# Block 0's A12*B21 as a nested seven-product unit, with the sums of W2, the loads of x and some stores moved to make room for it

## The chip, the cores and the metric

One NeuronCore of one Trainium2 chip. The metric is device microseconds of one execution of the whole program.

## The reference

```python
x: 16 x 512 x 768, w1: 768 x 3072, b1: 3072, w2: 3072 x 768     # float32
y = x @ w1 + b1
y = 0.5 * y * (1 + erf(y / sqrt(2)))
out = y @ w2
```

## The kernel before

The 8192 rows are eight blocks of 1024. In each block the two matmuls are done by Strassen-Winograd: seven products of half-size operands (numbered 1 to 7) in place of eight, at the price of sums of operands, which VectorE makes. From block 2 on the second matmul is nested: each of the seven products is itself made by seven products of quarter size. Block 0's second matmul has one level only, in four row units; block 1's is mixed: its products 1, 4 and 2 are nested units ("UnitH"), and four "lean" row units do the other four. Nesting saves an eighth of the matrix work and costs sums, buffers and DRAM traffic, for which blocks 0 and 1 have little room.

A row unit of blocks 0 and 1, and its stores (shortened):

```python
class Unit2:                                   # one 128-row unit; sb is the block
    def __init__(self, g, sb, u):
        self.lean = sb > 0
    def mm(self, p, dst, first, c0, c1):       # product p: 12 matmuls of 384 columns
        if self.lean and p in (1, 2, 4):
            return                             # these come from the nested units
        ...
    def right_done(self):                      # upper row's store
        nc.sync.dma_start(out=orr[...], in_=self.o[:, 0, c0:N])
    def left_done(self, row, bank):            # ... lower row's sum or copy, then its store
```

A nested unit, one product of half size made by seven of quarter size:

```python
class UnitH(Unit3):
    def mm(self, q, dst, first, c0, c1):       # 12 matmuls of 192 columns for each q
        for c in range(NQ):
            for t in range(2):
                nc.tensor.matmul(out=dst[:, t * N4:(t + 1) * N4], lhsT=a, rhs=self.w[q][:, c, :], ...)
```

Units are interlaced. A period issues the first products of unit i between the last ones of unit j; between them stand six "slots", in which other engines' work is put into the program order:

```python
p1(i); copy_xy(i)            # ScalarE copies the start value into bank bY
p7(j); fill(1); p5(i); fill(2); p3(j); fill(3); p6(i); j.right_done(); fill(4)
p4(j); fill(5); p2(i); fill(6)            # lean row units: p5(i) ahead of p7(j), no p1, p2, p4
```

## Time and profile before

| | |
|---|---|
| median of the first runs | 852.89 us (852.71 to 853.48) |
| TensorE busy | 845.5 of 850.6 us |
| first product of block 0's second matmul | at 120.01 us |
| first product of block 2 | at 224.67 us |

Columns of a timeline: start in us, duration in us, engine, line, operation, output<-input, count, and in brackets how long the engine was idle before it and what released it. bX, bY, bZ and bW are PSUM banks, "arena" is the kernel's SBUF, and SPq or ACTq is a transfer issued by SyncE or ScalarE. Starts are exact; a matmul's end is modelled, so for TensorE I take differences of starts. A matmul of 384 columns starts 162.5 ns after its predecessor, one of 192 columns 82.5 ns.

### The profile page before, as it was taken

The numbers are of one execution on the slowest core, as the hardware profiler recorded it, in microseconds if no ns is written. First come the engines' busy times: TensorE is split into PE (matmuls) and PEld (weight loads), VectorE is DVE, ScalarE is ACT, GpSimd is POOL, SyncE is SP. The second block draws the span as 40 slices with busy tenths as digits, with TensorE's granted clock in tenths as the row PEclk, the third lists the DMA queues.
The fourth block names the chain that finished last, engine by engine and source line by source line (L and its number), as shares of the span: only waits on it lengthen the run. The fifth ranks groups of instructions, "written<-read, shape, count | busy, mean of one in ns | idle before, by whom it ended". The sixth has DMA issues, their size and how long they took to land.

```text
span 850.6 us, 16487 instructions
## 1 busy us (share of the span) xinstructions
PE 845.5 (99%) x6432; PEld 569.6 (67%) x6432; DVE 667.2 (78%) x1126; ACT 421.3 (50%) x686; POOL 84.1 (10%) x135
## 2 busy tenths in 40 slices
PE   9999999999999999999999999999999999999998
PEld 5444446687544897449964499645995469944798
DVE  5766678786657998679976799768996699956998
ACT  4777761122277513773148822487216771267611
POOL 5021100002100002000020000210002100010000
PEclk9999999999999999999999999999999999999999
DMA  9998777659999699987999689995999949984398
GB/s 229 199 284 170 165 160 277 234 195 218 234 331 207 194 332 372 296 177 236 332 381 266 155 291 335 361 293 111 315 351 344 283 111 328 356 311 172 101 310 283
DMA packets 143522, 219.05 MB, mean 258 GB/s; under 512 B 61756, under 2 KB 84724, under 8 KB 143444
## 3 DMA queue, kind: packets, MB, share of 16 engines
q1 hardware_dynamic: 117824, 179.74, 67.3%
q0 software_dynamic: 25440, 38.15, 20.6%
q8 instruction: 50, 0.82, 0.4%
q14 instruction: 28, 0.23, 0.1%
q10 hardware_dynamic: 180, 0.11, 0.0%
HBM read 180.30 MB, written 47.87 MB: 268 GB/s over the span
## 4 chain that ended last, share of the span: by engine, by line
PE 95%; DMA 4%; DVE 0%; ACT 0%; issue 0%; POOL 0%; DVEq 0%; ACTq 0%
PE bY L388 21%; PE bY L493 15%; PE bX L388 14%; PE bX L493 10%; PE bZ L388 7%; PE bW L388 7%; PE bZ L493 5%; PE bW L493 5%; PE bY L432 5%; DMA arena<-in_x_dram 2%; PE bZ L432 2%; PE bW L432 2%; PE bX L432 2%; DMA arena<-in_w_dram 1%; PE bY L580 1%; PE bX L580 1%
## 5 line engine op out<-in xcount | busy, mean ns | idle before, releaser
L191 DVE TENSOR_TENSOR arena<-arena 128x768 f16<-128x768 f16 (+4 forms) x630 | 403.4, 671 | 7.5 <-PE bW L432 1.1
L388 PEld LDWEIGHTS <-arena 128*128 128x128 f16 x1974 | 192.6, 98 | 224.0 <-issue 0.4
L493 PEld LDWEIGHTS <-arena 128*128 128x128 f16 x3528 | 292.1, 98 | 8.4 <-issue 0.4
L388 PE MATMUL bY<-arena 128*128 128x512 f16 x846 | 214.4, 379 | 0.1
L613 DVE TENSOR_TENSOR arena<-bY,arena 128x512 f32<-128x512 f32 (+1 forms) x102 | 69.4, 681 | 127.0 <-PE bY L388 90.3
L493 PE MATMUL bY<-arena 128*128 128x192 f16 x1500 | 138.3, 246 | 0.0
L388 PE MATMUL bX<-arena 128*128 128x512 f16 x564 | 138.2, 379 | 0.0
L606 ACT COPY bY<-bX 128x512 f32<-128x512 f32 (+1 forms) x143 | 78.6, 550 | 119.4 <-DVE arena L542 82.0
L404 ACT ACTIVATE arena<-arena,b1t 128x1024 f16<-128x1024 f32 x94 | 108.0, 1149 | 54.0 <-DVE arena L641 54.0
L626 ACT COPY arena<-bW 128x512 f32<-128x512 f32 (+1 forms) x147 | 81.1, 552 | 90.7 <-PE bW L493 43.9
L493 PE MATMUL bX<-arena 128*128 128x192 f16 x1020 | 93.1, 246 | 0.1
L641 DVE TENSOR_TENSOR arena<-bZ,arena 128x512 f32<-128x512 f32 (+1 forms) x102 | 69.3, 679 | 22.2 <-PE bZ L388 18.2
L388 PE MATMUL bW<-arena 128*128 128x512 f16 x282 | 76.2, 379 | 0.0
L388 PE MATMUL bZ<-arena 128*128 128x512 f16 x282 | 76.2, 379 | 0.0
L432 PEld LDWEIGHTS <-arena 128*128 128x128 f16 x528 | 51.6, 98 | 34.1 <-issue 0.2
L525 POOL DMA_DIRECT2D out_dram<-arena x42 | 30.6, 729 | 406.4 <-DVE arena L637 370.2
L409 ACT ACTIVATE arena<-bX,b1t 128x512 f16<-128x512 f32 x94 | 64.0, 681 | 10.0 <-PE bX L388 10.0
L409 ACT ACTIVATE arena<-bY,b1t 128x512 f16<-128x512 f32 x94 | 63.4, 674 | 0.0
L657 ACT COPY bZ<-bY 128x512 f32<-128x512 f32 (+1 forms) x54 | 29.0, 537 | 65.7 <-DVE arena L641 31.4
L299 POOL DMA_DIRECT2D arena<-in_x_dram x60 | 32.7, 550 | 248.2 <-DMA arena<-arena 137.9
L493 PE MATMUL bW<-arena 128*128 128x192 f16 x504 | 48.4, 246 | 0.0
L493 PE MATMUL bZ<-arena 128*128 128x192 f16 x504 | 48.4, 246 | 0.0
(60 smaller groups left out, 401.8 us busy)
## 6 DMA issues: line engine op xcount, KB each, us to landing
arena<-w2s SPq DMA_DIRECT2D x294, 288.0 KB, 4.7
arena<-w1s SPq DMA_DIRECT2D x72, 672.0 KB, 7.0
out_dram<-arena POOLq DMA_DIRECT2D x42, 384.0 KB, 7.2
w2s<-arena SPq DMA_DIRECT2D x49, 288.0 KB, 3.8
arena<-in_x_dram POOLq DMA_DIRECT2D x60, 192.0 KB, 7.1
w1s<-arena SPq DMA_DIRECT2D x12, 672.0 KB, 6.1
arena<-in_w_dram POOLq DMA_DIRECT2D x17, 384.0 KB, 7.6
out_dram<-arena SPq DMA_DIRECT2D x17, 384.0 KB, 3.4
```

The source lines that it names most:

```text
L191: nc.vector.tensor_tensor(out=o, in0=a, in1=b, op=op)
L299: nc.gpsimd.dma_start(out=xhs[t], in_=xr[:, sb * 8 + t, :])
L388: nc.tensor.matmul(out=dst[:, 0:RH], lhsT=w1_op(self.wt, slot)[:, c, :], rhs=a[:, c, :], start=first and c == 0, stop=c == self.C - 1, ski ...
L404: nc.scalar.activation(out=self.G[1][:, hi, :, :], in_=self.tmp, func=GELU, bias=b1t[:, 2 * hi + 1:2 * hi + 2])
L409: nc.scalar.activation(out=self.G[0][:, hi, row, :], in_=bank[:, 0:RH], func=GELU, bias=b1t[:, 2 * hi:2 * hi + 1])
L432: nc.tensor.matmul(out=dst[:, 0:N2], lhsT=a, rhs=w[:, :, c, :], start=first and c == 0, stop=c == self.C - 1, skip_group_check=True)
L493: nc.tensor.matmul(out=dst[:, t * N4:(t + 1) * N4], lhsT=a, rhs=w[:, c, :], start=first and c == 0 and t == ts[0], stop=c == NQ - 1, skip_ ...
L525: eng.dma_start(out=orr[:, s0:s0 + 2, right * N2:(right + 1) * N2], in_=self.dst[:, r].rearrange("p t h n -> p t (h n)"))
L606: nc.scalar.copy(out=bY[u.g % 2][:, 0:u.F], in_=bX[u.g % 2][:, 0:u.F])
L613: nc.vector.tensor_tensor(out=u.c22(), in0=bY[u.g % 2][:, 0:u.F], in1=w[:, 0:u.F], op=ADD)
L626: nc.scalar.copy(out=w[:, 0:u.F], in_=bW[:, 0:u.F])
L641: nc.vector.tensor_tensor(out=u.c12(), in0=bZ[:, 0:u.F], in1=w[:, 0:u.F], op=ADD)
```

## The change

Its intent: leave out product 2 of block 0's four row units and make it once, nested, ahead of block 1's three nested units. That costs buffers and time on VectorE just there, so the sums of W2 (28 of them, stored to DRAM for the later blocks) are spread over block 1 with five more buffers; six of these sums are fetched back from DRAM when they are needed; block 2's x is loaded sooner; the lean units' stores go from SyncE's queue to ScalarE's; and block 0's four copies from bY to bZ go from VectorE to ScalarE.

```diff
-            for n, a, b in ((7, b22, b12), ...):
-                    puts.append(lambda: put(n, t[n]))
+            for n, a, b in ((7, b22, b12), ...):
+                    puts.append([LAG[0], lambda eng: put(n, t[n], eng)])     # stored LAG slots later
...
+        HYBRID = ((0, 2), (1, 1), (1, 4), (1, 2))                             # was (1, 4, 2), block 1 only
...
+                self.eng = nc.scalar if self.lean and u < 2 * NU - 1 else nc.sync
...
-                if self.lean and p in (1, 2, 4):
+                if p == 2 or self.lean and p in (1, 4):
                     return
...
-                    for p in (5, 6, 7, 3):
-                        split_w2(p)
-                    hyb_w[1] = split_w2(1)
+                    for p, t in ((6, (0, 1, 2, 3)), (1, (4, 5, 0, 1)), (4, (2, 3, 4, 5)), (2, (0, 1, 2, 5))):
+                        split_w2(p, t)
...
             if m == 0 and slot == 1:
-                hyb_w[4] = split_w2(4, ...)
+                load_w2s(1, (7, 4))
...
+            if m == 1 and slot == 6:
+                split_w2(7, (6, 7, 8, 9))
+                split_w2(5, (10, 6, 7, 8))
...
-                if m == 2:
+                if m == 1:
                     load_next_x(2, range(3))
+                if m == 3:
+                    for t in range(3):
+                        transpose_dma(2, t)
+                    load_next_x(2, range(3, 6))
...
+            if k == 0 and slot == 4:
+                LAG[0] = 3
+                split_w2(3, (1, 2, 3, 4))
...
-            on_act = ... (isinstance(u, Unit2) and u.lean) ...                # copy bY -> bZ
+            on_act = ... isinstance(u, Unit2) ...
```

More of the change, by code (lines that the diff above doesn't have):

```diff
@@ L152 @@
     tmps1 = [tmp_at(o_tmp + 4 * k * RH) for k in range(2)]
-    o_stage = o_wt + 2 * WT_N
+    o_stage = o_wt + 2 * N + PAR
     stage = [cut(o_stage + k * WB, WB, "p (c n) -> p c n", c=NQ)
@@ L164, with strip, wb_at @@
           for o in (o_x0 + W2_N, o_x0 + W2_N + GS_N, o_x1, o_x1 + GS_N)]
-    osbs = [cut(o, PAR).bitcast(FP32).rearrange("p (a n) -> p a n", a=2)
-            for o in (o_wt, o_x1 + 2 * GS_N)]
-    par1, par4 = [cut(o, PAR).bitcast(FP32).rearrange("p (r t h n) -> p r t h n", r=2, t=2, h=2)
-                  for o in (o_wt, o_x1 + 2 * GS_N)]
+    osbs = [[cut(o, n).bitcast(FP32) for o, n in zip(oo, (2 * N2, 2 * N))]
+            for oo in ((o_x1 + 2 * GS_N + 2 * N + 2 * N2, o_wt),
+                       (o_x1 + 2 * GS_N + 2 * N, o_x1 + 2 * GS_N))]
+    assert 2 * N + 4 * N2 <= PAR
+    par02, par1, par4 = [cut(o, PAR).bitcast(FP32).rearrange(
+        "p (r t h n) -> p r t h n", r=2, t=2, h=2) for o in (o_wt + 2 * N, 2 * XT_N, o_x1 + 2 * GS_N)]
     par11 = cut(o_w2, W2P).bitcast(FP32).rearrange("p (c n) -> p c n", c=NH)[:, 0:8, 0:N4].rearrange(
         "p (r t h) n -> p r t h n", r=2, t=2)
-    osbs1 = [cut(XT_N + k * PAR, PAR).bitcast(FP32).rearrange("p (a n) -> p a n", a=2)
-             for k in range(2)]
-    def lev_strip(c, r):
-        return [Gs[0][k // 2][:, c:c + NQ, k % 2, r:r + 2 * P] for k in range(4)]
+    osbs1 = [[cut(XT_N + k * PAR, 2 * N2).bitcast(FP32),
+              cut(XT_N + k * PAR + 2 * N2, 2 * N).bitcast(FP32)] for k in range(2)]
+    def strip(h, a, c, r):
+        return Gs[0][h][:, c:c + NQ, a, r:r + 2 * P]
+    def wb_at(off):
+        return cut(off, WB, "p (c n) -> p c n", c=NQ)
+    hyb_lev = [[strip(0, 0, 0, 0), strip(1, 1, 0, 0), Gs[0][1][:, 0:NQ, 0, 2 * P:RH], strip(1, 1, NQ, 0)],
+               [strip(0, 1, 0, 0), strip(0, 0, NQ, 0), strip(0, 1, NQ, 0), strip(0, 0, 0, 2 * P)],
+               [strip(0, 1, 0, 2 * P), strip(0, 0, NQ, 2 * P), strip(0, 1, NQ, 2 * P), strip(0, 0, 0, 0)],
+               [strip(0, 1, 0, 0), strip(0, 0, NQ, 0), strip(0, 1, NQ, 0), strip(0, 0, NQ, 2 * P)]]
+    spare = stage + [wb_at(2 * XT_N + o) for o in
+                     (PAR, PAR + WB, XT_N, XT_N + WB, XT_N + 2 * WB)]
+    hyb_w = {2: {7: stage[0], 5: stage[1], 6: stage[2], 4: stage[5]},
+             1: dict(zip((7, 4, 5, 6), map(wb_at, (o_x0 + W2_N, o_x0 + W2_N + WB, o_x1, o_x1 + WB)))),
+             4: {7: wb_at(o_x1), 4: wb_at(o_x1 + WB), 5: stage[3], 6: stage[4]}}
     b1t = wp.tile([P, 2 * NH], FP32, name="b1t")
@@ L244 @@
         SLOT = {1: B11, 2: B21, 3: B22, 4: T4, 5: T1, 6: T2, 7: T3}
-        staged = [0]
-        puts, raws = [], []
+        puts, raws, LAG = [], [], [2]
         def quarters(p):
@@ L250, in quarters, with split_w2, put @@
             return w[:, 0, 0:NQ, :], w[:, 1, 0:NQ, :], w[:, 0, NQ:NH, :], w[:, 1, NQ:NH, :]
-        def split_w2(p, t=None, q=None):
+        def split_w2(p, t, q=None):
             b11, b12, b21, b22 = quarters(p)
-            def put(q, src):
-                nc.sync.dma_start(out=w2s[p, q][:], in_=src)
-            if t is None:
-                t = {n: stage[(staged[0] + k) % len(stage)] for k, n in enumerate((7, 5, 6, 4))}
-                staged[0] += 4
+            def put(q, src, eng=nc.sync):
+                eng.dma_start(out=w2s[p, q][:], in_=src)
+            t = {n: spare[k] for n, k in zip((7, 5, 6, 4), t)}
             for n, a, b in ((7, b22, b12), (5, b12, b11), (6, b22, t[5]), (4, b21, t[6])):
@@ L264, in f, with load_w2s @@
                     tt(t[n], a, b, SUB)
-                    puts.append(lambda: put(n, t[n]))
+                    puts.append([LAG[0], lambda eng: put(n, t[n], eng)])
                 later(WB, f, slow if q is None else q)
-            return t
+        def load_w2s(p, qs):
+            for q in qs:
+                nc.sync.dma_start(out=hyb_w[p][q], in_=w2s[p, q][:])
         def raw_w2(p):
@@ L340, with operand @@
                    5: GA, 6: GB, 7: G1[:, :, 1, :]}
+        HYBRID = ((0, 2), (1, 1), (1, 4), (1, 2))
+        def operand(sb, p):
+            return OPERAND[p] if sb else Gs[0][1][:, :, 0, :]
         def half_sums(c, ks=(0, 1, 2)):
@@ L357, in lev_of, with lev_sums @@
             return lev[(i - 1) % 2] if i else lev0
-        def lev_sums(i, c0=0, c1=NQ, ks=(0, 1, 2, 3), q=None, p=None, levs=None):
-            A = OPERAND[ORDER[i] if p is None else p]
+        def lev_sums(i, c0=0, c1=NQ, ks=(0, 1, 2, 3), q=None, m=None):
+            A = OPERAND[ORDER[i]] if m is None else operand(*HYBRID[m])
+            levs = None if m is None else hyb_lev[m]
             a11, a12 = A[:, c0:c1, 0:2 * P], A[:, NQ + c0:NQ + c1, 0:2 * P]
@@ L428, in mm @@
                 for c in range(c0, c1):
-                    a = {1: G1[:, c, 0, r], 2: G2[:, c, 0, r], 4: G2[:, c, 1, r],
+                    a = {1: G1[:, c, 0, r], 4: G2[:, c, 1, r],
                          3: GS[3][:, c, :], 5: GS[0][:, c, :], 6: GS[1][:, c, :],
@@ L442, in c12 @@
             def c12(self):
-                return self.o[:, 0, N2:N]
+                return self.o[0]
             def c22(self):
-                return self.o[:, 1, N2:N]
+                return self.o[1][:, N2:N]
             def right_done(self):
-                c0 = N2 if self.lean else 0
-                nc.sync.dma_start(out=orr[:, self.sb * 8 + self.u, c0:N], in_=self.o[:, 0, c0:N])
+                self.eng.dma_start(out=orr[:, self.sb * 8 + self.u, N2:N], in_=self.o[0])
             def left_done(self, row, bank):
-                if self.lean and row == 0:
+                if row == 0:
+                    if not self.lean:
+                        nc.scalar.copy(out=self.rows(par02), in_=bank[:, 0:N2])
                     return
                 if self.lean:
-                    tt(self.o[:, 1, 0:N2], bank[:, 0:N2], self.rows(par4), ADD)
+                    tt(self.o[1][:, 0:N2], bank[:, 0:N2], self.rows(par4), ADD)
                 else:
-                    nc.scalar.copy(out=self.o[:, row, 0:N2], in_=bank[:, 0:N2])
-                if row == 1:
-                    nc.sync.dma_start(out=orr[:, self.sb * 8 + NU + self.u, :],
-                                      in_=self.o[:, 1, :])
+                    nc.scalar.copy(out=self.o[1][:, 0:N2], in_=bank[:, 0:N2])
+                self.eng.dma_start(out=orr[:, self.sb * 8 + NU + self.u, :], in_=self.o[1])
         units3 = {}
@@ L562, in __init__ @@
             def __init__(self, g, sb, m):
-                self.g, self.sb, self.p = g, sb, HYBRID[m]
+                self.g, (self.sb, self.p) = g, HYBRID[m]
                 self.lev, self.w = hyb_lev[m], dict(hyb_w[self.p])
@@ L566, in __init__ @@
                 self.w.update({1: b11, 2: b21, 3: b22})
-                self.add = par1 if self.p == 2 else None
-                self.dst = {1: par1, 4: par4, 2: par11}[self.p]
+                self.add = {0: par02, 1: par1}[self.sb] if self.p == 2 else None
+                self.dst = {1: par1, 4: par4, 2: par11}[self.p] if self.sb else par02
                 self.alloc = lambda: None
             def mm(self, q, dst, first, c0, c1):
-                A, s = OPERAND[self.p], self.lev
+                A, s = operand(self.sb, self.p), self.lev
                 for c in range(NQ):
@@ L590, in finish @@
                             in_=self.dst[:, n // 2, n % 2])
-        HYBRID = (1, 4, 2)
-        hyb_lev = [lev_strip(0, 0), lev_strip(NQ, 0), lev_strip(0, 2 * P)]
-        hyb_w = {}
-        def wb_at(off):
-            return cut(off, WB, "p (c n) -> p c n", c=NQ)
         def p1(u, c0, c1):
@@ L651, in p6 @@
             u.mm(6, bY[u.g % 2], False, 0, u.C)
-            on_act = isinstance(u, Unit3) or (isinstance(u, Unit2) and u.lean) or (isinstance(u, Unit1) and u.sb >= ONE and u.g % 2)
+            on_act = isinstance(u, Unit3) or isinstance(u, Unit2) or (isinstance(u, Unit1) and u.sb >= ONE and u.g % 2)
             if isinstance(u, Unit3) and u.add is not None:
@@ L930, in fill_mm1, with drain @@
                 flush(soon)
-        def drain(slot):
-            while puts:
-                puts.pop(0)()
+        def drain(slot, eng=nc.sync, wait=True):
+            for f in puts:
+                f[0] -= 1
+            while puts and not (wait and puts[0][0] > 0):
+                puts.pop(0)[1](eng)
             if slot > 1:
@@ L962, in fill_mm2_one @@
                 g_sum(1, U + 1, q=soon)
+            if U + 2 == NU and slot == 5:
+                lev_sums(None, m=0, ks=(0, 1, 3))
+            if U + 1 == NU and slot == 4:
+                lev_sums(None, m=0, ks=(2,))
             if U + 1 == NU and slot == 2:
-                lev_sums(None, p=HYBRID[0], levs=hyb_lev[0])
+                lev_sums(None, m=1, ks=(0, 1, 2))
             if slot > 1:
@@ L977, in fill_hyb @@
             if m == 0 and slot == 1:
-                o = (o_x0 + W2_N, o_x0 + W2_N + WB, o_wt + PAR, o_wt + PAR + WB)
-                hyb_w[4] = split_w2(4, dict(zip((5, 6, 7, 4), map(wb_at, o))), queue)
-                lev_sums(None, p=HYBRID[1], levs=hyb_lev[1])
-            if m == 1 and slot == 1:
-                lev_sums(None, p=HYBRID[2], levs=hyb_lev[2])
-                o = (o_x1, o_x1 + WB)
-                hyb_w[2] = split_w2(2, dict(zip((5, 6, 7, 4), [wb_at(k) for k in o] +
-                                                [stage[staged[0] % len(stage)], hyb_w[1][7]])), queue)
-            if m == 2 and slot == 2:
+                load_w2s(1, (7, 4))
+                lev_sums(None, m=1, ks=(3,))
+            if m == 0 and slot == 4:
+                load_w2s(1, (5, 6))
+            if m == 0 and slot == 5:
+                lev_sums(None, m=2)
+            if m == 1 and slot == 5:
+                lev_sums(None, m=3, ks=(0, 1))
+            if m == 1 and slot == 6:
+                split_w2(7, (6, 7, 8, 9))
+                split_w2(5, (10, 6, 7, 8))
+            if (m, slot) in ((1, 6), (2, 1), (2, 3), (2, 5), (3, 1), (3, 5)):
+                slow.pop(0)[1]()
+            if m == 2 and slot == 1:
+                load_w2s(4, (7, 4))
+                lev_sums(None, m=3, ks=(2,))
+            if m == 2 and slot == 5:
+                lev_sums(None, m=3, ks=(3,))
+            if m == 3 and slot == 2:
                 for k in (0, 1):
@@ L1008, in fill_lean @@
                 g_sum(1, U + 1, q=soon)
+            if k == 0 and slot == 4:
+                LAG[0] = 3
+                split_w2(3, (1, 2, 3, 4))
             if slot > 1:
                 sums(1200)
-            if k == 0 and slot == 6:
-                for t in range(3):
-                    transpose_dma(2, t)
-                load_next_x(2, range(3, 6))
+            if slow and slot in (2, 5):
+                slow.pop(0)[1]()
             if k == 1 and slot == 2:
@@ L1017, in fill_lean @@
                     load_wt(2 * NH + n)
-            if k == 1 and slot == 4:
+            if k == 0 and slot == 6:
                 for t in range(3, 6):
@@ L1021, in fill_lean @@
                 load_next_x(2, range(6, 8))
-            if k == 2 and slot == 4:
+            if k == 1 and slot == 6:
                 for t in range(6, 8):
                     transpose_dma(2, t)
-            if k == 3 and slot == 4:
+            if k == 3 and slot == 3:
                 x_sums(2, soon)
@@ L1032, in fill_lean @@
                 flush(queue)
-                drain(slot)
+                flush(slow)
+                drain(slot, wait=False)
         def fill_mm2_two(sb, k, slot):
```

## The prediction

> **What bounds the kernel now**
>
> I read the page's busy table first, then the chain of waits, then a table by stretch, and only then the order of time inside the stretch that the change touches.
>
> ```profile
> PE 845.5 (99%) x6432; PEld 569.6 (67%) x6432; DVE 667.2 (78%) x1126; ACT 421.3 (50%) x686; POOL 84.1 (10%) x135
> ...
> PE 95%; DMA 4%; DVE 0%; ACT 0%; issue 0%; POOL 0%; DVEq 0%; ACTq 0%
> ```
>
> TensorE is busy for 845.5 of 850.6 us, and the chain that ended last is 95% TensorE. The 4% of DMA are the loads at the very start, before TensorE has anything to multiply. "Busy" alone would not prove much, because an engine can be busy and still late. So I cut the span where one block hands over to the next and asked each stretch for its sum:
>
> ```profile
> core 0: us, PE busy (x) PEld busy (x) DVE busy (x) ACT busy (x) POOL busy (x), PEclk, DMA share, GB/s
> ...
> 120.17:168.91 48.74, 48.74 (x298) 29.05 (x297) 37.55 (x54) 9.01 (x17) 0.00 (x0) 1.00 0.70 245
> 168.91:195.56 26.65, 26.65 (x279) 23.52 (x277) 22.44 (x32) 7.59 (x16) 1.61 (x3) 1.00 0.56 181
> 195.56:224.84 29.28, 29.28 (x193) 18.42 (x192) 18.76 (x27) 4.75 (x10) 6.85 (x12) 1.00 1.00 210
> 224.84:845.80 620.96, 620.87 (x5052) 440.36 (x5051) 507.02 (x866) 315.87 (x517) 50.95 (x80) 1.00 0.89 274
> ```
>
> The first three rows are what the change touches: the second product of block 0 (120 to 169 us), the three nested products of block 1 (169 to 196) and block 1's four lean row units (196 to 225). TensorE fills each of them to the hundredth, at the full clock, and loses 0.09 us in all that follows up to 845.8. No hidden wait is to be won back. VectorE has 11.2, 4.2 and 10.5 us free in the three stretches. So the only gain is matrix work that disappears, and every wait that the new order brings is paid in full, because there is no slack to hide it in.
>
> The chain of waits in order of time gives the price of that matrix work (start, duration, what):
>
> ```profile
> 165.01 3.90 PE bY L432 x24
> 168.91 1.95 PE bX L432 x12
> 170.86 0.99 PE bX L580 x12
> 171.85 1.95 PE bY L432 x12
> ...
> 179.68 1.98 PE bX L580 x24
> ```
>
> A product over 384 columns costs 3.90/24 = 162.5 ns a matmul; a nested quarter product over 192 columns costs 1.98/24 = 82.5 ns. These start-to-start figures are the ones to use: the 326 and 246 ns of the groups include the pipeline's drain.
>
> **What the Trainium skill says**
>
> "TensorE: Matmul & The Clock Gate", section "Wait — 56ns, not 53.3ns?": back-to-back matmuls on a warm array start N / 2.4 GHz + about 2.5 ns apart. For 384 and 192 columns that is 162.5 and 82.5 ns, exactly what this trace shows. The 2.5 ns matter here: a nested product has more, shorter matmuls, so they eat into the saving of an eighth.
>
> "DMA: Bandwidth & Descriptors", section "Anatomy of one DMA — SWDGE (gpsimd) path": about 2.0 us fixed plus bytes / 436 GB/s, and semaphore waits are made by the issuing sequencer before dispatch. A 288 KB quarter of W2 would be 2.0 + 0.7 = 2.7 us (an estimate from that page, whose fit is for the other issue path). In the trace the stores of such quarters, issued by SyncE, land in 2.1/2.9/5.0 us (min/median/max), the loads in block 2 and later, with DMA nearly full, in 2.7/4.7/9.5. So it agrees for quiet queues only; for a loaded queue I use the 4.7. The second statement means that a DMA waiting on SyncE's queue holds up all behind it.
>
> **The change part by part**
>
> 1. *Removed from TensorE.* Block 0's row units no longer multiply A12 by B21. That is 4 units x 12 matmuls x 162.5 ns = 7.80 us.
>
> 2. *Added to TensorE.* A fourth nested unit does the same quarter product for all four row units: 7 products x 12 matmuls x 82.5 ns = 6.93 us. The instruction order confirms it: 48 matmuls of 384 columns fewer, 84 of 192 columns more, nothing else changed on TensorE. Net: 7.80 - 6.93 = 0.87 us less, all of it on the path that sets the end. This is 0.10% of 852.89.
>
> 3. *VectorE.* Four more level sums of 1536 elements (950 ns) = 3.8 us; six more evictions with an add for the new unit, about 555 ns each = 3.3 us; four copies of 560 ns from bY to bZ go to ScalarE = -2.2 us. Sum about +4.9 us. The three stretches then hold 37.55 + 22.44 + 18.76 + 4.9 = 83.7 us in 104.67 - 0.87 = 103.8, or 81%. In block 2's second half (the same table for 285 to 336 us) VectorE runs for 48.65 of 51 us and TensorE still fills all 51, so 81% is bearable on average. The 28 sums of W2 are as many as before, at some 0.7 us each, but 16 in place of 20 stand in block 0 and 12 in place of 8 in block 1, now spread over more units. The fullest period I find is unit 2 of block 0: six W2 sums (4.2), four row sums (3.3), two evictions (1.1), two level sums (1.9) = 10.5 of its new 11.7 us. It fits, barely.
>
> 4. *ScalarE.* Six more copies of about 0.47 us (2.8 us), and all eight stores of the lean units, 8 x 0.34 us of issue (the time they take in SyncE's queue) = 2.7 us, where ScalarE was 4.75 of 29.28 us busy. Off the path, unless a store that waits for VectorE's sum holds up the copy of the next start value into bY; that copy has three products of 1.95 us until it is needed.
>
> 5. *DMA.* Six more loads of 288 KB (W2 sums fetched back from DRAM), 1.7 MB more in all. Bytes are not the matter; their deadlines are. The tightest: unit 1 of the nested ones needs quarter 5 at its p5. Shifting the old times by 7.80 us, the last row unit's p3 ends at 168.9; its sum on VectorE and SyncE's store before the load cost 1.2 us and 0.4 us in the old trace, so the load goes out near 170.5. p5 follows p6, p4, p2, p1 and p7 of the new order (0.99 + 1.95 + 3 x 0.99), at 174.85. That leaves 4.3 us for a landing of 2.9 (quiet) to 4.7 (full). The DMA share there was 0.56 and no x load has begun yet, so I expect it in time, with some chance of a wait of up to about 0.5 us. All other fetched quarters have over 5 us to spare because SyncE's queue runs ahead of TensorE.
>
> 6. *Sooner x of block 2.* Its first loads go out near 179 in place of 190, and all transposes come one unit earlier. The old order met block 2 with a wait of 0.06 us (a product of 2.01 in place of 1.95 us at 225.5), so this wins at most that. The first W1 load of block 2 now stands behind the last store of a W2 sum in the buffer it overwrites: out near 205 in place of 200, 7 us to land, needed at 224. Harmless.
>
> Sum: -0.87 from TensorE, -0.05 at the hand-over, +0.15 for an expected share of waits: about -0.8 us.
>
> **The rivals**
>
> *The late fetch.* Quarter 5 arrives after its p5 and TensorE waits; the same for any other fetched quarter if SyncE's queue stands still behind a store. For: the margin of 1.4 to -0.4 us above; stores of raw quarters in block 0 took up to 7.9 us to land. Against: the share of DMA is low just there. It would give back 0.3 to 1 us: 852.3 to 853.
>
> *VectorE falls behind.* The sums reuse six stage buffers at distances down to four, while each store is now held back by two slots. If VectorE waits for such a store, the sums after it are late, bZ isn't cleared, and TensorE stops. For: 10.5 of 11.7 us in unit 2. Against: a store issued two slots of 1.95 us late and 2.9 us in flight takes 6.8 us, four slots are 7.8; and before, with five buffers, VectorE showed no wait for a DMA in that stretch. It would cost 0.5 to 2 us: 852.5 to 854.
>
> *A real gain beyond the matrix work.* Spreading the sums and taking the stores off SyncE's queue would pay only if TensorE had waited there. The table by stretch says it did not. To be 2% faster 17 us would have to vanish; nothing in the profile offers even one.
>
> *Contention carried into block 2*, from moved stores, x loads and W2 sums sharing the queues between 196 and 225 us, where the DMA share was 1.00. For: that share. Against: the deadlines there are long, over 10 us for W1. It could cost 1 us or so.
>
> **Range and chances**
>
> 852.89 - 0.8 = 852.1. The runs of before spread by 0.77 us (852.71 to 853.48), so half of that must be allowed on both sides: low 851.5. Above, one of the small waits may come true and the draw may be high: 853.2. Both ends are far from 2%. Slower by over 2% would need 17 us of new waits, twenty times what the tightest deadline can cost; I leave 1% for an overlap of buffers that I misjudged. Faster by over 2% gets half a percent.
>
> **What would show it right or wrong**
>
> In the changed profile TensorE should have 36 more matmuls, and about 0.9 us less between the start of block 0's second product (120.17) and block 2's first product (224.84). If the table by stretch shows TensorE filled to the hundredth there again, step 2 is right and no rival came true. The first product of the nested units should start near 163.1, the lean units near 194.7. If a product of nested unit 1 into bW shows more than 0.99 us, with the W2 fetch as what ended the wait, the late fetch is the rival that counts; if VectorE's sums wait for a store into the W2 scratch, it is the second. VectorE's busy time should rise to about 672 us. The prediction would be wrong if block 2 and later, which the change leaves alone, took another time than 621 us, or if TensorE's clock were not granted in full.

## The result, and the profile after

| | before | changed |
|---|---|---|
| first runs, median | 852.89 us | 852.22 us (851.87, 852.09, 852.34 and 854.49) |
| second chip, median | 852.50 us (9 runs) | 851.72 us (851.35 to 852.95, 5 runs) |
| ratio, first | | 0.9996 (95% interval 0.9979 to 1.0014) |
| ratio, second chip | | 0.9993 (0.9980 to 1.0006) |

A ratio is the mean time of one kernel's runs over that of the other's of the same rounds, so not quite the ratio of the medians. By the ratios the two kernels are the same; the medians differ by 0.67 and 0.78 us, where 0.8 was predicted. One execution, 854.49, lies 2 us above the others, and it is the one that was profiled first. That is a piece of luck: it shows the risk that the change brought in. The profile of the unaltered changed kernel on the second chip shows a usual execution (851.63 us).

The usual execution first: its busy table, and its table by stretch, cut at the first product of 384 columns, the first nested one, the lean units and block 2.

```profile
PE 843.8 (99%) x6468; PEld 571.1 (67%) x6468; DVE 671.1 (79%) x1132; ACT 423.2 (50%) x692; POOL 86.1 (10%) x139
```

```profile
120.32:163.22 42.90, 42.90 (x263) 25.54 (x262) 38.59 (x53) 10.64 (x22) 0.00 (x0) 1.00 0.75 260
163.22:194.80 31.58, 31.58 (x349) 29.23 (x348) 21.73 (x33) 8.44 (x18) 3.96 (x8) 1.00 0.70 191
194.80:224.12 29.32, 29.32 (x195) 18.46 (x193) 22.54 (x33) 4.61 (x10) 6.92 (x12) 1.00 1.04 238
224.12:845.82 621.70, 621.70 (x5066) 441.33 (x5063) 507.96 (x869) 315.59 (x517) 50.71 (x80) 1.00 0.88 276
```

TensorE has 36 more matmuls than before and is again busy to the hundredth in every stretch. The last row ends at the start of the last matmul, the prediction's last row about one product earlier, so their lengths do not compare; by starts, block 2's first product to the last matmul took 622.05 us before, 621.70 here and 622.10 in b_sync (below). The distance that matters is from the first product of block 0's second matmul to block 2's first product. The timelines of TensorE give it: before,

```profile
120.01 2.11 PE L432 MATMUL bX<-arena 128*128 128x384 f16 x12
...
224.67 0.81 PE L388 MATMUL bX<-arena 128*128 128x512 f16 x3
```

and the usual execution of the changed kernel,

```profile
120.32 2.11 PE L454 MATMUL bX<-arena 128*128 128x384 f16 x12
...
224.12 0.81 PE L409 MATMUL bX<-arena 128*128 128x512 f16 x3
```

(104.66 by these rounded starts, 104.67 unrounded) against 103.80: 0.87 us less, the predicted figure. Its start differs by up to 0.5 us between the profiles (120.01 to 120.56), ahead of all that the change touches. So the two spans differ by 0.78 us (850.64 and 849.86) as the sum of +0.32 at the start, -0.87 here, -0.35 in block 2 and later, and +0.12 after the last matmul. Only the -0.87 is the change's work. That the others nearly cancel, and the medians differ by almost the predicted 0.8, is luck.

Now the slow execution. Two lines of its waits of TensorE (who waited for whom, us in total, times, longest), and then the chain that ended last in the lean units (start, duration, what):

```profile
PE bY L409 <- ACT bY L620: 1.2, 2, 0.8
PE bY L454 <- ACT bY L618: 1.2, 1, 1.2
```

```profile
202.89 1.80 PE bY L454 x11
...
210.48 11.95 DMA w2s<-arena
...
222.50 0.34 ACTq L482
...
222.88 0.49 ACT bY L618
```

TensorE's product at 223.41 waited for ScalarE's copy of a start value into bY (line 618). That copy was late because ScalarE stood, from 216.87 on, at the issue of two stores: of the first (line 471) until 219.62, of the second (line 482) until 222.50. The second waited for a quarter of W2, sent to DRAM from SyncE's queue, to land, which took 11.95 us. The stores neither read nor write anything of that quarter. ScalarE's own timeline shows the copy's wait; SyncE's queue, below it, shows most of why the quarter took so long:

```profile
216.41 0.46 ACT L671 COPY bZ<-bY 128x384 f32<-128x384 f32 x1 [4.50 <-PE bY L454]
219.62 0.34 ACTq L471 DMA_DIRECT2D out_dram<-arena  x1
222.50 0.34 ACTq L482 DMA_DIRECT2D out_dram<-arena  x1
222.88 0.48 ACT L618 COPY bY<-arena 128x384 f32<-128x384 f32 x1 [6.00 <-DMA w2s<-arena]
```

```profile
209.50 0.89 SPq L234 DMA_DIRECT2D arena<-w1s  x2
210.48 0.41 SPq L271 DMA_DIRECT2D w2s<-arena  x1
210.98 12.44 SPq L320 DMA_TRANSPOSE arena<-arena  x2
```

The quarter was issued 1 us after two W1 tiles of 672 KB. In the packets of the trace the W1 tiles moved from 210.6 to 219.1 and the quarter from 216.1 to 220.2: it stood behind them. The last 2.2 us came after its own packets. In the trace's completion records, 11 of its 16 shares (each transfer has 16 such records) had landed by 220.73, the other five only between 222.16 and 222.42; in a_again, the usual execution, all 16 landed from 219.76 to 219.88. What held the five is not shown.

Why does a store on ScalarE wait for it at all? The compiled program answers. Transfers issued by SyncE and ScalarE share eight completion semaphores, given out in turn, and a transfer that gets a semaphore waits for the transfer that had it before. From the compiled program, in order, with the semaphore of each (the wait is for its last holder, eight back):

```
SyncE    W1 load              semaphore 2
SyncE    W1 load              semaphore 3
SyncE    W2 quarter to DRAM   semaphore 4      <- landed at 222.4
ScalarE  store L471           semaphore 5
SyncE    x transposes         semaphores 6, 7
ScalarE  store L482           semaphore 0
SyncE    W2 quarters          semaphores 1, 2
ScalarE  store L471           semaphore 3      waits for the second W1 load
ScalarE  store L482           semaphore 4      waits for the W2 quarter
```

Both stores' waits fit: the W1 loads' packets ended at 219.1, the first store went out at 219.62. On SyncE's queue such a wait holds up other transfers. On ScalarE it holds up copies that TensorE needs.

### The profile page after: what moved, and what is told of

Read it like the earlier page. It is cut to its first block, busy times and chain, and to the rows that moved or that the text cites. A ratio compares the mean times of both kernels' runs of the same rounds, so it can differ in the third digit from the quotient of the medians.

```text
span 852.7 us, 16579 instructions
## 1 busy us (share of the span) xinstructions
PE 844.6 (99%) x6468; PEld 571.2 (67%) x6468; DVE 671.4 (79%) x1132; ACT 422.8 (50%) x692; POOL 85.9 (10%) x139
## 4 chain that ended last, share of the span: by engine, by line
PE 92%; DMA 6%; DVE 1%; issue 0%; ACT 0%; POOL 0%; ACTq 0%; DVEq 0%
PE bY L409 21%; PE bY L514 15%; PE bX L409 14%; PE bX L514 10%; PE bZ L409 7%; PE bW L409 7%; PE bW L514 5%; PE bZ L514 5%; PE bY L454 3%; DMA arena<-in_x_dram 3%; DMA w2s<-arena 1%; PE bY L601 1%; DMA arena<-in_w_dram 1%; PE bW L454 1%; PE bX L601 1%; PE bZ L454 1%
## 5 line engine op out<-in xcount | busy, mean ns | idle before, releaser
L206 DVE TENSOR_TENSOR arena<-arena 128x1536 f16<-128x1536 f16 (+6 forms) x634 | 406.5, 672 | 7.8 <-DMA arena<-arena 1.3
L671 ACT COPY bZ<-bY 128x512 f32<-128x512 f32 (+1 forms) x58 | 30.8, 532 | 70.8 <-DVE arena L655 27.5
```

Of the source, the lines that this page charges most:

```text
L206: nc.vector.tensor_tensor(out=o, in0=a, in1=b, op=op)
L671: nc.scalar.copy(out=bZ[:, 0:u.F], in_=bY[u.g % 2][:, 0:u.F])
```

## The experiments

All stand against the kernel before on the same chip (medians 852.50 to 852.60); "changed" is the unaltered changed kernel, 851.72 on the same chip as the first eight runs.

### The changed kernel again, and its stores elsewhere

The changed kernel unaltered (a_again); the lean stores back on SyncE (b_sync); on GpSimd (c_pool):

```diff
-                self.eng = nc.scalar if self.lean and u < 2 * NU - 1 else nc.sync
+                self.eng = nc.sync                                  # b_sync
+                self.eng = nc.gpsimd if self.lean else nc.sync      # c_pool
```

> The changed kernel unaltered, to see how often it shows the slow execution. Theory A (ScalarE's stores wait for a transfer of SyncE's queue each time, TensorE loses some 2 us whenever that transfer is slow): the runs spread, most 0.5 to 1 us under the kernel before, some 1 to 2 us over it; the profiled one shows ScalarE's copy for the lean units held by a transfer for over 1 us. Theory B (the execution of 854.49 was a chance disturbance): nearly all runs within 0.4 us of 852.0 and the profile shows no TensorE wait in the lean units.

> Only the lean units' stores go back from ScalarE to SyncE. Theory A: TensorE has no wait in the lean units, all runs 851.5 to 852.2, 0.9 us under the kernel before, because a store that waits for a transfer now holds SyncE alone. Theory B: no difference from the unaltered changed kernel, medians within 0.2 us. A third way: with stores and W2 puts in one queue the x transposes of block 2 come late and TensorE waits at block 2's first product, up to 2 us more.

> Only the lean units' stores go from ScalarE to the idle GpSimd. Theory A: as with SyncE, 851.5 to 852.2 and no wait of ScalarE for a transfer. If a store to DRAM in that window costs TensorE by contention and not by ScalarE's waiting, the wait stays, about 2 us in the profile. Risk: block 2's x loads stand behind the stores on GpSimd's queue and come later by some 1.5 us; over 10 us of slack, so no cost.

Measured: a_again 851.72 us (851.35 to 852.95), b_sync 851.83 (851.67 to 852.52), c_pool 852.51 (851.68 to 853.07). In the profile of a_again ScalarE waits again for the W2 quarter:

```profile
ACT bY L618 <- DMA w2s<-arena: 3.5, 1, 3.5
```

but TensorE does not wait. So both theories were half right: the wait of ScalarE is there each time, and it reaches TensorE only in a slow execution. In b_sync's profile no ScalarE wait for a transfer is left, and the distance is 103.80 us again; the time is the same. Moving these stores to ScalarE therefore bought nothing. In c_pool the wait of ScalarE is gone too, yet TensorE waits 0.4 us for a sum on VectorE at block 2's start, and VectorE had waited 2.5 us for a transfer; I did expect no cost there. Its runs are 0.7 us over the other two in the median, within their spread.

### The two prices

The removed product: in d_p1twice each of block 0's four units repeats its product 1, which has the same shape, in the place of the removed one. The added product: in f_nest2 each matmul of the new nested unit is made twice, the copy into unused PSUM. Results right in both.

```diff
         def p2(u):
+            if isinstance(u, Unit2) and not u.lean:
+                u.mm(1, bX[u.g % 2], True, 0, u.C)                  # d_p1twice
...
+                        if self.sb == 0:                             # f_nest2, in UnitH.mm
+                            nc.tensor.matmul(out=<unused PSUM>, lhsT=a, rhs=self.w[q][:, c, :], start=True, stop=True)
```

> The price of the removed product by itself: block 0's four units repeat their first product (same shape, 12 matmuls of 384 columns each) where the removed one stood; the result stays right. Step 1 of the prediction: 4 x 12 x 162.5 ns = +7.80 us over the changed kernel, so about 859.8, whatever the lean units do. If other engines had been the bound in block 0 it would cost less than that; if TensorE waited there, the profile would show it.

> The price of the added nested product: each of block 0's 84 nested matmuls is made twice, the second copy into PSUM that is otherwise free; result right. Step 2 of the prediction: 84 x 82.5 ns = +6.93 us over the changed kernel, 858.6 to 859.3, all of it between the first nested matmul and the lean units. If the nested unit were bound by VectorE or by its fetched W2 quarters, twice its matmuls would hide some of that and the cost would be under 6.5.

Measured: d_p1twice 860.83 us, f_nest2 858.74. By the starts of TensorE the distance to block 2's first product is 111.60 in d_p1twice (120.33 to 231.93), and 110.72 in f_nest2 (120.37 to 231.09):

```profile
231.93 0.81 PE L409 MATMUL bX<-arena 128*128 128x512 f16 x3
```

```profile
231.09 0.81 PE L409 MATMUL bX<-arena 128*128 128x512 f16 x3
```

That is 7.80 and 6.92 over the changed kernel's 103.80: both prices are as worked out. f_nest2's time of +7.0 agrees. d_p1twice's is +9.1, 1.3 more than its matmuls. In its profile 1.1 us of that lie after the last matmul (5.12 us from its start to the end of the span, 4.04 in the changed kernel), where only the last stores run. I don't know why, and leave it open.

### Making ScalarE's wait longer

To see whether ScalarE's wait really costs TensorE, the transfers ahead of ScalarE's store were made slower, without changing their number or the order within each queue: the first W1 load of block 2 is twice as large, its copy going into the next tile, which is loaded rightly afterwards. That second load must wait for the first to land (in h_load_act it went out at 220.28, 10.5 us after the first), and by the compiled program the semaphores fall to other transfers than before. Once with the lean stores on ScalarE (h_load_act), once on SyncE (i_load_sync).

```diff
             if k == 1 and slot == 2:
-                for n in range(2):
-                    load_wt(2 * NH + n)
+                nc.sync.dma_start(out=<tiles 24 and 25>, in_=w1s[hi_of(2 * NH)][:].unsqueeze(1).broadcast_to([P, 2, WT_N]))
+                load_wt(2 * NH + 1)
```

> The changed kernel with the first W1 load of block 2 made twice as large (its copy goes into the next tile, which is then loaded rightly), so that SyncE's transfers land some 4 to 8 us later; ScalarE keeps the lean stores. Theory A (a store on ScalarE waits for the landing of a transfer of SyncE's queue issued eight transfers before, and everything behind it on ScalarE waits too): ScalarE's wait for a transfer grows from 3.5 to 6 us to 8 us or more, TensorE waits 2 us or more for ScalarE's copy in the lean units, 854 to 857. Theory B (chance): like the next run, under 1 us apart.

> The same larger W1 load with the lean stores on SyncE. Theory A: ScalarE has no wait for a transfer, TensorE loses nothing in the lean units; what it may lose is at block 2's start, where W1 or the x transposes come late, 0 to 2 us. 851.7 to 854, at least 1.5 us under the run with ScalarE's stores. Theory B: the two are within 0.5 us.

Measured: h_load_act 854.09 us (852.25 to 857.68), i_load_sync 853.39 (851.95 to 853.97). The medians are 0.7 us apart, less than the 1.5 expected, and the runs overlap: the times alone do not tell the two apart. The profiles do. In h_load_act, whose profiled execution was the slowest (857.68), ScalarE's and TensorE's waits are

```profile
ACT bY L618 <- DMA arena<-w1s: 8.1, 1, 8.1
...
PE bY L454 <- ACT bY L618: 3.3, 1, 3.3
```

This time the semaphore's last holder was the second W1 load, as the compiled program says. In i_load_sync's profile ScalarE has no wait for a transfer, the distance is 103.80, and TensorE waits 0.9 us later, for W1 itself. So the mechanism is shown by the profiles, and its size depends on the execution.

The same waits in two runs that are described below, k_latex and l_bz_dve:

```profile
222.75 0.48 ACT L618 COPY bY<-arena 128x384 f32<-128x384 f32 x1 [5.84 <-DMA arena<-arena]
223.29 2.11 PE L454 MATMUL bY<-arena 128*128 128x384 f16 x12 [1.03 <-ACT bY L618]
```

```profile
221.28 0.48 ACT L618 COPY bY<-arena 128x384 f32<-128x384 f32 x1 [4.37 <-DMA w2s<-arena]
```

Taken together, five profiles give the slack (the wait of ScalarE's copy at line 618, then TensorE's wait for that copy, us):

| profile | ScalarE waits | TensorE waits | difference |
|---|---|---|---|
| a_again | 3.53 | 0 | |
| l_bz_dve (below) | 4.37 | 0 | |
| k_latex (below) | 5.84 | 1.03 | 4.81 |
| changed, slow execution | 6.00 | 1.19 | 4.81 |
| h_load_act | 8.13 | 3.31 | 4.82 |

ScalarE has 4.8 us for such a wait, and each microsecond more is TensorE's. Had the quarter's last five shares landed with the others, at 220.73, ScalarE's wait in the slow execution would have been 4.3 us (an estimate: 6.00 less 1.69), under these 4.8: by this estimate TensorE's first stop came of those last 1.7 us.

The profile of h_load_act shows a second cost. After TensorE's stop, these columns: stretch, length and busy time of each engine, then the granted clock (third from the end):

```profile
216.00:222.00 6.00, 6.00 (x39) 3.62 (x37) 4.36 (x6) 0.46 (x1) 0.00 (x0) 1.00 0.57 177
222.00:225.00 3.00, 0.20 (x2) 0.00 (x0) 1.42 (x2) 0.02 (x1) 0.00 (x0) 0.89 1.04 298
225.00:228.00 3.00, 2.48 (x8) 1.13 (x8) 1.22 (x2) 0.87 (x2) 1.22 (x3) 0.50 1.12 347
228.00:231.00 3.00, 3.00 (x10) 1.26 (x9) 2.81 (x4) 0.63 (x2) 0.37 (x1) 0.50 1.07 250
```

The same view, cut where the clock changes:

```profile
222.04:224.31 2.27, 0.16 (x1) 0.00 (x0) 1.42 (x2) 0.00 (x0) 0.00 (x0) 1.00 0.96 291
224.31:231.14 6.83, 5.62 (x17) 2.45 (x17) 4.03 (x5) 1.66 (x4) 1.59 (x3) 0.50 1.10 296
```

From 224.31 on, before TensorE resumed at 225.52, the clock is granted by half, and for over 5 us each matmul takes twice as long. The Trainium skill, "TensorE: Matmul & The Clock Gate", section "What's actually happening", says that the array falls to half its clock after at least one idle window of about 3.4 us, and that these windows run free of what the kernel does. The traces agree on the length: the clock stayed halved for 3.41 us in g2_block0 and 6.83 in h_load_act and k_latex, one or two such windows. Stops of 3.3, 4.2 and 4.6 us were followed by half clock, stops of 1.2 us weren't. But a whole idle window was not needed: here the clock fell 2.3 us after TensorE's next matmul was due (222.04), so that in the 3.41 us before the fall TensorE was still busy for the first 1.1. Of the 5.32 us by which block 2's first product came later (109.12 against 103.80) 3.48 are the stop by the starts, the other 1.84 the halved clock, and some more falls in block 2.

### Undoing the spread of the W2 sums

All 28 sums in block 0 again, in the six buffers that the nested product leaves there.

```diff
-                    for p, t in ((6, (0, 1, 2, 3)), (1, (4, 5, 0, 1)), (4, (2, 3, 4, 5)), (2, (0, 1, 2, 5))):
+                    for p, t in ((7, (0, 1, 2, 3)), (5, (4, 5, 0, 1)), (3, (2, 3, 4, 5)),
+                                 (6, (0, 1, 2, 3)), (1, (4, 5, 0, 1)), (4, (2, 3, 4, 5)), (2, (0, 1, 2, 5))):
...                                          # and out of their slots in block 1; g2_block0 also alters when the stores go out
```

> Undoes the spreading: all 28 sums of W2 stand in block 0 again, in the six stage buffers that the nested product leaves there; the rest is as in the changed kernel. If VectorE is full there (prediction: 10.5 of 11.7 us in unit 2, and the sums need 8 us more), TensorE waits 1 to 5 us in block 0 or the first nested unit: 852.8 to 857. If the spreading is not needed for TensorE: 851.5 to 852.2, like the changed kernel.

> Undoes the spreading of the W2 sums as before, mended: in the last run stores were put behind the next writer of their buffer, which gave the wrong result; now each store is issued before its buffer is written again. All 28 sums in block 0, six buffers. If VectorE is the bound there: TensorE waits for its sums 2 to 8 us around the first nested unit, 854 to 860. If the waits of the last run came of its wrong order alone: 851.5 to 852.5.

g_block0 gave a WRONG result (relative error 1.5): with the change's delay of two slots, stores were issued in program order behind the next sum into the same buffer. Its 860.74 us prove nothing, and it was mended as g2_block0, with a delay of one slot and a store between any two of the last sums: right, 857.82 us. In its profile TensorE stops for VectorE in the new nested unit:

```profile
170.67 2.08 PE L601 MATMUL bW<-arena 128*128 128x192 f16 x12 [4.21 <-DVE arena L206]
```

In the 7.35 us around it (163.35 to 170.70) VectorE was busy for 7.25 us, TensorE for 3.14, and for 3.3 us after it the clock was granted by half. The distance to block 2's first product is 109.76 us, 5.96 over the changed kernel's: 4.38 are the stop by the starts, the other 1.58 the halved clock. So the spreading is worth 6 us against this order of the sums, where the nested product is there, as its condition and not as a gain.

### Block 2's x as late as before

```diff
-                if m == 1:
-                    load_next_x(2, range(3))
-                if m == 3:
-                    for t in range(3):
-                        transpose_dma(2, t)
-                    load_next_x(2, range(3, 6))
+                if m == 3:
+                    load_next_x(2, range(3))
...                                          # the transposes, too, and block 2's x sums, in their old slots
```

> The changed kernel with the x loads and transposes of block 2 as late as before. By the prediction the sooner x is worth 0.05 us at most: 851.5 to 852.2. If the W2 sums in the lean units make the transposes late in SyncE's queue, TensorE waits at block 2's first products, 1 to 4 us.

Measured: 860.34 us, 8.6 over the changed kernel's median (of the other chip), 7.7 over the kernel before on its own. The prediction's 0.05 us were far off. TensorE's timeline at block 2's start and VectorE's before it:

```profile
232.62 1.44 PE L409 MATMUL bW<-arena 128*128 128x512 f16 x3 [4.56 <-DVE arena L206]
233.85 4.04 PE L454 MATMUL bZ<-arena 128*128 128x384 f16 x12
```

```profile
223.64 0.55 DVE L206 TENSOR_TENSOR arena<-bY,arena 128x384 f32<-128x384 f32 x1
231.61 3.76 DVE L206 TENSOR_TENSOR arena<-arena 128x1536 f16<-128x1536 f16 x4 [7.42 <-DMA out_dram<-arena]
```

The sums of block 2's x wait 7.4 us. The profile names a store as the last wait, but by the compiled program these sums wait for the x transposes, the last of which landed at 231.53 (the store at 231.36). SyncE issued its last transposes only between 224.0 and 229.3, where the kernel before issued them between 218.9 and 222.1. With the W2 stores of the lean units in SyncE's queue and x late, the transposes come five microseconds late; TensorE stops for 4.6 us and loses half its clock for the next 5. SyncE's W1 loads waited 4.9 us for a W2 store, and its last transposes 6.0 us for x loads, which had themselves waited up to 9.9 us for earlier transposes; how much of the 8.6 us each of these costs was not tested.

### Two parts by themselves

Block 0's four copies back from ScalarE to VectorE (l_bz_dve), and the kernel before with nothing but its lean stores on ScalarE (j_before_act):

```diff
-            on_act = isinstance(u, Unit3) or isinstance(u, Unit2) or ...
+            on_act = isinstance(u, Unit3) or (isinstance(u, Unit2) and u.lean) or ...        # l_bz_dve
...
-                nc.sync.dma_start(out=orr[...], in_=self.o[:, 0, c0:N])                      # j_before_act
+                eng = nc.scalar if self.lean else nc.sync                                    # (both stores)
+                eng.dma_start(out=orr[...], in_=self.o[:, 0, c0:N])
```

> Block 0's four copies from bY to bZ go back to VectorE (4 x 0.56 us), all else as changed. If VectorE's slack in block 0 is as worked out (10.5 of 11.7 us in the fullest unit, now 11.1): nothing, 851.5 to 852.3. If it is less: TensorE waits up to 1 us in block 0.

> The kernel before with one part of the change alone: its lean units' stores on ScalarE. By theory A each of these stores waits for the landing of the transfer issued eight before it, but in this kernel no W2 store stands behind W1 loads there, so ScalarE should wait under 4 us and TensorE not at all: 852.2 to 852.9, as the kernel before. If a store on ScalarE costs TensorE time by itself (its issue, or a wait for VectorE's sum): over 853.

Measured: l_bz_dve 851.53 us (851.41 to 851.70) against 852.60 before, distance 103.79: moving the copies bought nothing that shows. j_before_act 852.55 against 852.60, distance 104.67, ScalarE's longest wait for a transfer 1.4 us: without W2 stores behind W1 loads, ScalarE's stores neither help nor harm.

No version beat the changed kernel beyond the spread. l_bz_dve and b_sync are level with it. In b_sync no copy of ScalarE can stand behind a store, which takes away the way in which the slow execution came about; five runs are too few to show that slow executions become rarer.

## Why the prediction was right or wrong

The time was right (852.1 predicted, 852.22 and 851.72 measured), and so was the reason that carries it; that the times agree to 0.1 us is partly luck, as the sum of the spans above shows.

- *Steps 1 and 2, the price of the products.* Right to the hundredth: -7.80 and +6.93 worked out, 7.80 and 6.92 measured separately, -0.87 together.
- *Step 3, VectorE.* Busy time 671.1 us where 672 was expected (+3.9, not +4.9), block 0's stretch holds 38.59 of 42.90 us. "It fits, barely" was too careful: with the four copies back on VectorE it still fitted. But eight us of sums more didn't.
- *Step 4, ScalarE.* This step failed in part. It named the right instruction, the copy of the start value into bY, and the wrong thing for its store to wait for. Not VectorE's sum but a transfer on another engine's queue held it, through a shared completion semaphore, and no rival on my list was that. "Contention carried into block 2" came nearest, but i_load_sync moves more bytes through the lean units without a stop there: crowding delays the transfer, and TensorE pays because ScalarE waits for it. The slack of three products (5.85 us) measured 4.8. The wait stays under the slack in the usual execution and cost 2.4 us of stops in the slow one (1.19, 0.38 and 0.81).
- *Step 5, the fetched quarters.* Right: the tightest was issued at 170.21 (170.5 expected), such fetches landed in 2.8 to 3.4 us, its product started at 174.90 without a wait. The rival of the late fetch didn't happen.
- *Step 6, sooner x.* Wrong in its reasoning, though the sum didn't show it. I priced it against the kernel before, where it would have been worth 0.05 us. In the changed order it is what keeps 8 us of stop and half clock away. And the W1 load behind a W2 store, called "harmless", went out at 211.09 in the usual execution and 209.50 in the slow one, not at 205, and W2 quarters and transposes stood behind it. That is where ScalarE's long wait began.
- *The rival "VectorE falls behind"* didn't come true in the changed kernel, and g2_block0 shows that it would have without the spreading, by 6 us and not by 0.5 to 2: the stop alone was 4.4 us, twice what I allowed, and I had left out the clock, which added 1.6.
- *Signs of being wrong.* In the usual execution none came: the first nested product started at 163.22 (163.1 expected), the lean units at 194.80 (194.7), block 2 and later took 621.70 us where 622.05 by the same cut before, and the clock was granted in full.
- *Range.* 852.1 and its range rest on the usual execution. Single executions went outside it on both sides, 851.35 and 854.49. Two of nine (854.49 and 852.95) were over 852.5; for the second there is no trace, so its cause is open.

Open too: why the W2 quarter landed in 11.9 us in one execution and within 7.8 in another. Both stood behind the same W1 loads. The last 1.7 us of the slow one are those of the five late shares.

## What to carry to other kernels

Where one engine is busy to the hundredth, price a change by that engine's instructions, and check it by the distance between two of its instructions in the trace; it measured 0.87 us where the times of whole executions could not tell it from nothing. Parts that make room for a change can have no gain of their own and still be its conditions, so price each by what happens without it in the new order, not in the old one: here the spread sums and the sooner x were conditions (6 and 8.6 us), the moved stores and copies were not, and the six fetched sums were not tested by themselves. Put transfers on a queue whose engine does nothing urgent: an engine that issues a transfer can wait for another queue's transfer that shares nothing with it but a semaphore.

## What the Trainium skill lacked or had wrong

- "DMA: Bandwidth & Descriptors", section "Issuing engines are not separate DMA queues", says that starting transfers on several engines saves only the time to start them. The runs agree (851.72 us with the stores on ScalarE, 851.83 on SyncE). It lacks the reverse risk: ScalarE waited 3.5 to 8.1 us at a store for an unrelated transfer of SyncE's queue. No page read tells of the eight completion semaphores that the compiled program gives out in turn.
- The same page, section "Anatomy of one DMA — SWDGE (gpsimd) path", fits a transfer's time by 2.0 us plus bytes / 436 GB/s, measured on GpSimd's path: an estimate of 2.7 us for 288 KB. A quarter behind two loads of 672 KB landed after 7.8 and 11.9 us; a term for what is ahead in the queue is lacking.
- "TensorE: Matmul & The Clock Gate", section "What's actually happening", has the clock fall after at least one idle window of about 3.4 us. In h_load_act it fell 2.3 us after TensorE had stopped, so less than a whole idle window was enough in this one stop. The halved clock then cost 1.8 us up to block 2's first product, beside the stop's own 3.5.
